# Queueing a kernel's side loads behind its weight loads, in a two-layer hybrid transformer block on one core

## The chip, the cores and the metric

The kernel runs on one NeuronCore of a Trainium2 chip. The metric is device time in microseconds (us). TensorE multiplies (PE in the profile, its weight loads PEld), VectorE (DVE), ScalarE (ACT) and GpSimd (POOL) do the elementwise work, and SyncE (SP) issues most of the transfers from HBM. Each engine executes its own queue of instructions in order. An instruction that waits holds up all that stands behind it on the same queue, and that is true of the queue in which SP issues transfers too.

## What is computed

Two layers over 512 tokens of `x` and 256 tokens of context, each 1024 wide. A layer normalises and modulates its input, projects it, feeds three branches, and merges them:

```
h = rms_norm(x, norm_w) * (1 + scale) + shift          # shift, scale, gate = silu(c) @ w_ada + b_ada
a_qkv, a_z, .., b_q, b_kv, b_z, c_qkv, c_z, merge = split(h @ w_in)
y_a = gated_head_rmsnorm(bidir_delta(...), a_z)        # branch A: gated delta rule, both directions
y_b = window_attention(...) * silu(b_z)                # branch B: attention in windows
y_c = retention_out(bidir_retention(...), c_z)         # branch C: retention, both directions
merged = sum over r of sigmoid(merge_r) * (y_r @ w_branch[r])
x = x + gate * (merged @ w_out)                        # the context likewise, in layer 0 alone
```

Branch A inverts a triangular matrix per chunk and head. After the second layer a last rms_norm gives the output.

## The kernel before

**Products.** Activations and weights are each split into a rounded part and a remainder (`hi`, `lo`), and a product is three passes on TensorE (`prod`, L261). A block of weights of 1024 x 128 is brought by `weight` (L300): SP loads it into one of two buffers `wr`, ACT rounds it into one of two `wh` (L282), POOL subtracts to get one of two `wl` in four instructions (L291). So a load of weights must wait until the block two before it has been split, and the split must wait until the product that last used its `wh` and `wl` is done. `weight` is traced with a higher priority, so that its load and split are placed well ahead of their product.

**Memory.** All other tiles are 36 slots in SBUF. `alloc` takes the slot that has been free longest, `free` gives it back. A load into a slot must wait until the last instruction that used the slot has finished. The matmul results go to eight banks in PSUM: two `px` (512 columns), one `pc` (256 columns), five general ones, `pg` (`gps`).

**Order.** The program is traced once, in the order of the code, and a planner then places each instruction on its engine's queue by priority and by the times that it reckons. On the chip that order is fixed.

**Fillers.** The projections for the gates (24 for `merge`, named `m`, and 12 named `az`, `bz`, `cz`) depend on `h` alone. `aside` (generator `self.fill`) computes them one at a time between the steps of slower chains, applies tanh (L282), and stores them to HBM as `kept`. `FILL[l]` says how many are traced in which stage: in layer 1 six beside the first inversion, 2, 4, 9 and 6 beside branch A's further stages (the 9 beside the second inversion `delta_inv`, the 6 beside the second `delta_chain`), then one in each of the eight steps of attention and one before branch C. `load` (L1243) brings a stored gate back into a slot when a branch or the merge needs it.

**The second inversion.** `delta_inv` runs 31 steps of two DVE instructions each (L288, scratch slot `ts`), then two transposes (L751, L752), sixteen DVE copies (L767) and twelve ACT copies. The ACT copies are queued behind the tanh of the filler two before (`issue_after(self.asides[-back][1])`, BACK[1] = (2, 2)). `levels` then sends bursts of small matmuls to TensorE (L795), which need all the copies.

**Branch A's end, branch B, merge.** After the second chain, `gated` (L926) brings `az`, and `branch_b` brings two tables (L1170) before its projections. The merge runs three rounds (r = 0, 1, 2 for branches A, B, C) of eight products; each is multiplied by its gate and added up. The output loop runs eight products with `w_out`, each in two halves (`out`: first half into `px`, second into `pc`), and adds the old `x` (loaded at L1381). The second halves of the last two blocks are held back until the rms of the first half has been traced.

Of the kernel before, what the change touches and what calls it, by code (L numbers as in the profile page):

```python
# [9 lines left out]
F32 = mybir.dt.float32  # L10
# [152 lines left out]
class Builder:  # L163
# [114 lines left out]
                last = i.name  # L278


    def act(self, out, in_, func, **k):
        return self.nc.scalar.activation(out, in_, func, **k)  # L282

# [10 lines left out]
    def weight(self, dram, kb=KB):  # L294
        nc = self.nc
        w = self.wr.tile([128, KB, 128], F32, name="wr")[:, 0:kb]
        hi = self.wh.tile([128, KB, 128], F32R, name="wh")[:, 0:kb]
        lo = self.wl.tile([128, KB, 128], F32R, name="wl")[:, 0:kb]
        with self.tc.high_priority(offset=WHI):
            nc.sync.dma_start(w, dram)  # L300
            self.act(hi, w, AF.Copy)
            for k in range(0, kb, 2):
                self.gtt(lo[:, k:k + 2], w[:, k:k + 2], hi[:, k:k + 2].bitcast(F32), ALU.subtract)
        return [hi[:, k] for k in range(kb)], [lo[:, k] for k in range(kb)]
# [86 lines left out]
    def ada(self, todo, ahead=1, begin=False):  # L391


        nc = self.nc

        def load(l, vec, mod, j):
            ss = [self.alloc() for _ in range(3)]
            for i in range(3):
                n = min(3, KB - 3 * i)
                nc.sync.dma_start(ss[i].f[:, 0:n * 256].rearrange("p (a b) -> p a b", a=n),  # L400
                                  self.a["wada"][l, j][:, 3 * i:3 * i + n])
            return ss

        held = deque(load(*t) for t in todo[:ahead])
        for i, (l, vec, mod, j) in enumerate(todo):
            if i + ahead < len(todo):
                held.append(load(*todo[i + ahead]))
            ss = held.popleft()
            ps = self.gps(256)
            for k in range(KB):  # L410
                g = k % 4 * 32
                nc.tensor.matmul(ps[g:g + 32], lhsT=self.csil[:, k],  # L412
                                 rhs=ss[k // 3].f[:, k % 3 * 256:k % 3 * 256 + 256],
                                 start=(k < 4), stop=(k >= 4), tile_position=(0, g))
            self.free(*ss)
            t = self.alloc()
            if begin:
                nc.vector.tensor_copy(t.f[:, 0:256], ps)
            else:
                self.act(t.f[:, 0:256], ps, AF.Copy)  # L420
            pst = self.gps(4)
            for m in range(2):
                self.mm(pst[:, m * 2:m * 2 + 2], t.f[:, m * 128:(m + 1) * 128], self.sel)
            self.free(t)
            c = slice(j, j + 9, 8) if j < 8 else slice(2 * j, 2 * j + 2)
            o, b = mod[:, c], vec[:, 8:32][:, c]
            self.tt(o, pst.rearrange("p (a b) -> p a b", b=2), b.unsqueeze(2).to_broadcast([128, 2, 2]), ALU.add)
            if j < 8:
                o = mod[:, 8 + j]
                self.stt(o, o, 1.0, vec[:, j:j + 1].to_broadcast([128, 2]), ALU.add, ALU.mult)  # L430
            else:
                nc.vector.tensor_scalar(out=o, in0=o, scalar1=0.5, scalar2=None, op0=ALU.mult)
            yield
# [732 lines left out]
    def branch_b(self, l, row, vb, last):  # L1166
        nc = self.nc
        tabs = [self.alloc(), self.alloc()]
        for i in range(2):
            nc.sync.dma_start(tabs[i].f[:, 0:512], self.a["tabs"][i])  # L1170
        cos, sin = tabs[0].f[:, 0:512], tabs[1].f[:, 0:512]
        n = SEQ if last else TOK
        kr = self.alloc()
        px, pc = self.pblk(l, "bk", True)
        self.rope(px, cos, sin, kr, 32)
        self.act(kr.f[:, SEQ:TOK], pc, AF.Copy)
        ks = []
        for g in range(2):
            kh, kl = self.alloc(True), self.alloc(True)
            src, same, other = kr.f[g * 64:g * 64 + 64], slice(g * 64, g * 64 + 64), slice(64 - g * 64, 128 - g * 64)  # L1180
            for o in (same, other):
                self.act(kh.r[o], src, AF.Copy, scale=0.125)
            for o in (same, other):
                self.stt(kl.r[o], src, 0.125, kh.f[same], ALU.mult, ALU.subtract)
            ks.append((kh, kl))
        self.free(kr)
        ns = self.st.tile([128, 8], F32, name="ns%d" % l, tag="ns")
        nc.vector.tensor_scalar(out=ns, in0=row[:, 16:24], scalar1=-1.0, scalar2=None, op0=ALU.mult)
        zs = []
        for g in range(2):  # L1190
            q = []
            for b in (2 * g, 2 * g + 1):
                px, pc = self.pblk(l, "bq%d" % b, not last)
                qr = self.alloc()
                self.rope(px, cos, sin, qr, 32)
                if not last:
                    self.act(qr.f[:, SEQ:TOK], pc, AF.Copy)
                for e in range(2):
                    t = self.alloc(True)
                    h, o = slice(e * 64, e * 64 + 64), slice(64 - e * 64, 128 - e * 64)  # L1200
                    self.act(t.r[h, 0:n], qr.f[h, 0:n], AF.Copy)
                    self.tt(t.r[o, 0:n], qr.f[h, 0:n], t.f[h, 0:n], ALU.subtract)
                    q.append(t)
                self.free(qr)
            if g:
                self.free(*tabs)
            z = [self.load("bz%d" % b, n) for b in (2 * g, 2 * g + 1)]
            for c in range(4 if last else 6):
                with self.tc.high_priority(offset=HI):
                    self.attn(c, g, q, *ks[g], vb, ns, z)  # L1210
                for _ in seq(take(self.mods, 1), take(self.fill, FILL[l][5])):
                    pass
            self.free(*q, *ks[g])
            zs.extend(z)
        return zs
# [23 lines left out]
    def load(self, nm, n):  # L1239
        while nm not in self.kept:  # L1240
            next(self.fill)
        s = self.alloc()
        self.nc.sync.dma_start(s.f[:, 0:n], self.kept[nm])  # L1243
        return s


    def layer(self, l, xs, rs, mod, vec, row, ada):
        nc = self.nc
        last = l == self.depth - 1
        n = SEQ if last else TOK  # L1250
# [75 lines left out]
        rc = self.ret_consts(l, row)  # L1326
        tabs = [self.alloc(), self.alloc()]
        for i in range(2):
            nc.sync.dma_start(tabs[i].f[:, 0:512], self.a["tabs"][2 + i])
        oc = [self.ret_head(l, h, rc, tabs, vt, last) for h in range(4)]  # L1330
        for h in range(4):
            self.tap("oc%d_%d" % (l, h), oc[h].f[:, 0:n])
# [2 lines left out]
        yc = [self.gated(l, oc[h], "cz%d" % h, nw[:, h:h + 1], not last) for h in range(4)]  # L1335
# [1 line left out]
            pass  # L1337
        m = []
        for r, y in enumerate((ya, yb, yc)):
            if r == 2:  # L1340
                y = [self.ysplit(t, n) for t in y]
            for h in range(4):
                self.tap("y%d_%d_%d" % (l, r, h), y[h][0].f[:, 0:n])
            for d in range(8):
                th = self.load("m%d_%d" % (r, d), n)
                px, pc = self.proj(self.a["wbr"][l, d, r], y, not last)
                self.stt(th.f[:, 0:SEQ], th.f[:, 0:SEQ], 1.0, px, ALU.add, ALU.mult)
                if not last:
                    self.stt(th.f[:, SEQ:TOK], th.f[:, SEQ:TOK], 1.0, pc, ALU.add, ALU.mult)
                if r:  # L1350
                    self.tt(m[d].f[:, 0:n], m[d].f[:, 0:n], th.f[:, 0:n], ALU.add)
                    self.free(th)
                else:
                    m.append(th)
            for t in y:
                self.free(*t)
# [11 lines left out]
        def out(d, w, i):  # L1368
            sl = parts[i]
            if i == 0:  # L1370
                ps = self.px.tile([128, 512], F32, name="px")[:, 0:sl.stop]
            else:
                ps = self.pc.tile([128, 512], F32, name="pc")[:, 0:256]
            self.prod(ps, w, self.hs, sl)
            x = new[d].f[:, sl]
            j = int(sl.start >= SEQ)
            self.stt(x, ps, mod[:, 16 + d, j:j + 1], x, ALU.mult, ALU.add)

        for d in range(KB):
            w = self.weight(self.a["wout"][l, d])  # L1380
            nc.sync.dma_start(new[d].f[:, 0:n], self.xd[d] if l else self.a["xT"][d][:, 0:n])  # L1381
            out(d, w, 0)
            if d < KB - 2:
                out(d, w, 1)
            else:
                held.append((d, w))
# [118 lines left out]
```

## Time and profile before

| | |
|---|---|
| median of 3 runs | 1809.99 us (1809.49 to 1810.56) |
| the profiled execution: its time | 1805.86 us |
| the profiled execution: its span, first to last instruction | 1803.7 us |
| mean granted TensorE clock | 0.984 of full speed |
| TensorE busy | 1704.5 us, 95% of the span |
| DVE, ACT, POOL busy | 1060.1, 844.6, 595.5 us |

A row of the timeline reads: start in us, length in us, engine and line, operation, output<-input, shapes, how many were merged (x), and in brackets the time that the engine sat idle before, with what ended the wait. A `q` behind an engine's name is its queue (SPq). Successive matmuls overlap, so that the last one of a row ends after the next has begun.

### The profile page before, as it was taken

Reading aid. Unit: us, or ns where it says so; the run is one execution under the profiler, and the core shown is the slowest. Engines: PE = TensorE matmul, PEld = TensorE weight load, DVE = VectorE, ACT = ScalarE, POOL = GpSimd, SP = SyncE. Lnnn points to the kernel's source line nnn. Section 1 sums busy time; section 2 is a strip of 40 time slices with the busy share of each in tenths; the row PEclk is TensorE's granted clock in tenths of the full one; section 3 lists DMA queues with packets and bytes.
Section 4 is the critical chain, followed back from the end, with each engine's and each line's share of the span. In section 5 each row is a group of like instructions: output and inputs, shape, how many; then the busy total and the mean of one; then the engine's idle time right before and its main releaser. Section 6 shows DMA issues by size and latency. Waiting matters only on the chain. (4 is left out here: it accounts for less than half of the span.)

```text
span 1803.7 us, 30670 instructions
## 1 busy us (share of the span) xinstructions
PE 1704.5 (95%) x11574; PEld 1449.5 (80%) x11574; DVE 1060.1 (59%) x2531; ACT 844.6 (47%) x2018; POOL 595.5 (33%) x739
## 2 busy tenths in 40 slices
PE   7999989999999999999999899979989999999997
PEld 3788879889877778988888697858778777888786
DVE  4668758633565464346563647966934767445653
ACT  6565545253554455222233556455354655433244
POOL 2422422312321213121453623433433422322563
PEclk9999999999999999999999999989999999999999
DMA  8211202313235234014453112201333432212552
GB/s 310 84 33 68 85 34 69 122 60 107 102 123 163 97 112 138 33 48 152 134 174 116 59 36 77 88 31 65 120 110 111 132 114 71 88 53 78 164 167 78
DMA packets 73748, 180.67 MB, mean 100 GB/s; under 512 B 8832, under 2 KB 16384, under 8 KB 73600
## 3 DMA queue, kind: packets, MB, share of 16 engines
q1 hardware_dynamic: 62144, 154.07, 26.5%
q10 hardware_dynamic: 11456, 24.65, 3.6%
q8 instruction: 91, 1.49, 0.4%
q14 instruction: 57, 0.47, 0.1%
HBM read 150.89 MB, written 27.79 MB: 99 GB/s over the span
## 5 line engine op out<-in xcount | busy, mean ns | idle before, releaser
L291 POOL TENSOR_TENSOR wl<-wr,wh 128x256 fp32r<-128x256 f32 x640 | 508.3, 825 | 1021.4 <-ACT wh L282 770.5
L261 PE MATMUL px<-hh,wh 128*128 128x512 f32 (+1 forms) x1000 | 393.0, 397 | 19.4 <-ACT wh L282 10.4
L261 PE MATMUL px<-hl,wh 128*128 128x512 f32 (+1 forms) x1000 | 393.4, 396 | 4.4 <-DVE hl L285 3.0
L282 ACT ACTIVATE wh<-wr 128x1024 fp32r<-128x1024 f32 (+1 forms) x184 | 174.3, 947 | 246.0 <-PE pc L261 101.5
L288 DVE TENSOR_TENSOR t<-t,t 128x512 f32<-128x512 f32 (+21 forms) x411 | 258.6, 630 | 41.0 <-ACT t L282 27.7
L261 PE MATMUL px<-hh,wl 128*128 128x512 f32 (+1 forms) x1000 | 263.2, 393 | 0.0
L282 ACT ACTIVATE t<-t 32x192 f32<-32x192 f32 (+10 forms) x314 | 167.4, 547 | 179.0 <-DVE t L285 127.4
L261 PE MATMUL pg<-t,t 128*128 128x128 f32 (+2 forms) x1616 | 230.3, 285 | 11.6 <-DVE t L288 11.3
L261 PEld LDWEIGHTS px<-hh,wh 128*128 128x128 f32 x1000 | 190.4, 191 | 58.4 <-ACT wh L282 11.0
L261 PEld LDWEIGHTS pg<-t,t 128*128 128x128 f32 x1616 | 205.5, 191 | 33.7 <-issue 11.4
L261 PEld LDWEIGHTS px<-hl,wh 128*128 128x128 f32 x1000 | 191.4, 191 | 41.9 <-DVE hl L285 7.5
L261 PEld LDWEIGHTS px<-hh,wl 128*128 128x128 f32 x1000 | 181.4, 190 | 33.2 <-issue 1.2
L261 PE MATMUL pc<-hh,wh 128*128 128x256 f32 x656 | 165.6, 287 | 3.7 <-DVE t L285 3.7
L261 PE MATMUL pc<-hl,wh 128*128 128x256 f32 x656 | 166.7, 289 | 2.0 <-DVE hl L285 2.0
L261 PEld LDWEIGHTS pc<-hh,wh 128*128 128x128 f32 x656 | 125.9, 192 | 8.4 <-DVE t L285 4.1
L261 PEld LDWEIGHTS pc<-hl,wh 128*128 128x128 f32 x656 | 126.2, 192 | 6.7 <-DVE hl L285 3.2
L282 ACT ACTIVATE t<-pg 128x128 f32<-128x128 f32 (+4 forms) x216 | 77.8, 384 | 110.5 <-PE pg L412 39.7
L261 PE MATMUL px<-t,wh 128*128 128x512 f32 x384 | 101.1, 401 | 4.5 <-DVE t L285 4.2
L282 ACT ACTIVATE t<-px 128x128 f32<-128x128 f32 (+2 forms) x120 | 54.7, 466 | 91.9 <-PE px L261 85.8
L261 PE MATMUL pc<-hh,wl 128*128 128x256 f32 x656 | 96.5, 287 | 0.0
L261 PEld LDWEIGHTS pc<-hh,wl 128*128 128x128 f32 x656 | 86.6, 194 | 0.9 <-issue 0.8
L261 PE MATMUL px<-t,hh 128*128 128x272 f32 (+1 forms) x384 | 86.5, 313 | 0.3 <-DVE t L285 0.3
(192 smaller groups left out, 2511.3 us busy)
## 6 DMA issues: line engine op xcount, KB each, us to landing
wr<-wblk SPq DMA_DIRECT2D x120, 512.0 KB, 3.3
t<-wada SPq DMA_DIRECT2D x48, 384.0 KB, 4.7
wr<-wbr SPq DMA_DIRECT2D x48, 256.0 KB, 2.7
m<-kept ACTq DMA_DIRECT2D x24, 384.0 KB, 2.3
t<-m SPq DMA_DIRECT2D x24, 384.0 KB, 3.4
wr<-wout SPq DMA_DIRECT2D x16, 512.0 KB, 3.3
t<-wada SPq DMA_DIRECT2D x24, 256.0 KB, 5.3
m<-kept ACTq DMA_DIRECT2D x24, 256.0 KB, 2.0
```

The lines of the kernel that those rows point to most:

```text
L261: return self.nc.tensor.matmul(out, lhsT=lhsT, rhs=rhs, start=start, stop=stop)
L282: return self.nc.scalar.activation(out, in_, func, **k)
L288: self.nc.vector.tensor_tensor(out=out, in0=in0, in1=in1, op=op)
L291: self.nc.gpsimd.tensor_tensor(out=out, in0=in0, in1=in1, op=op)
```

## The change

Four edits. `weight` keeps the instruction of its load as `self.fetch`. A new helper `bring` starts a load on SP, queued behind the load of whichever weights were traced last; it is used for stored gates (`load`), for modulation weights (`ada`, outside the start of the program), for the tables of branches B and C, and for the old `x` in the output loop. It sets an order of issue on SP's queue and waits for nothing else. The second output halves take a general bank (`gps`) in place of `pc`. Branch C's `ysplit` is traced at the start of round r = 1 in place of r = 2.

```
+    def bring(self, out, in_):
+        with self.tc.issue_after(self.fetch):
+            self.nc.sync.dma_start(out, in_)
...
         with self.tc.high_priority(offset=WHI):
-            nc.sync.dma_start(w, dram)
+            self.fetch = nc.sync.dma_start(w, dram).ins
...
-                nc.sync.dma_start(ss[i].f[:, 0:n * 256].rearrange("p (a b) -> p a b", a=n),
-                                  self.a["wada"][l, j][:, 3 * i:3 * i + n])
+                put = nc.sync.dma_start if begin else self.bring
+                put(ss[i].f[:, 0:n * 256].rearrange("p (a b) -> p a b", a=n),
+                    self.a["wada"][l, j][:, 3 * i:3 * i + n])
...
-            nc.sync.dma_start(tabs[i].f[:, 0:512], self.a["tabs"][i])
+            self.bring(tabs[i].f[:, 0:512], self.a["tabs"][i])
...
-        self.nc.sync.dma_start(s.f[:, 0:n], self.kept[nm])
+        self.bring(s.f[:, 0:n], self.kept[nm])
...
-            nc.sync.dma_start(tabs[i].f[:, 0:512], self.a["tabs"][2 + i])
+            self.bring(tabs[i].f[:, 0:512], self.a["tabs"][2 + i])
...
         for r, y in enumerate((ya, yb, yc)):
-            if r == 2:
-                y = [self.ysplit(t, n) for t in y]
+            if r == 1:
+                yc[:] = [self.ysplit(t, n) for t in yc]
...
             else:
-                ps = self.pc.tile([128, 512], F32, name="pc")[:, 0:256]
+                ps = self.gps(256)
...
-            nc.sync.dma_start(new[d].f[:, 0:n], self.xd[d] if l else self.a["xT"][d][:, 0:n])
+            self.bring(new[d].f[:, 0:n], self.xd[d] if l else self.a["xT"][d][:, 0:n])
```

## Rows read from the trace of the kernel before

**Rows 1.** Page, part 1: busy time, share of span, instructions.
```profile
PE 1704.5 (95%) x11574; PEld 1449.5 (80%) x11574; DVE 1060.1 (59%) x2531; ACT 844.6 (47%) x2018; POOL 595.5 (33%) x739
```

**Rows 2.** Waits of TensorE, whole span: total us, times, longest.
```profile
PE px L261 <- ACT wh L282: 10.7, 2, 10.4
...
PE px L261 <- ACT kept L282: 6.3, 1, 6.3
```

**Rows 3.** Chain that ended last, 1283 to 1315 us: start, us, what.
```profile
1289.60 0.86 DVE t L288
...
1297.94 0.40 DVE t L288
...
1304.71 0.33 SPq L1243
...
1310.73 8.50 PE px L261 x24
```

**Rows 4.** Waits of SP's queue, 1286 to 1311 us.
```profile
SPq L1243 <- DVE t L288: 18.2, 1, 18.2
```

**Rows 5.** Windows: length, busy PE, PEld, DVE, ACT, POOL; granted clock; DMA share; GB/s.
```profile
1293.42:1298.86 5.44, 5.44 (x26) 4.50 (x24) 5.13 (x10) 0.60 (x1) 3.50 (x4) 1.00 0.13 48
1304.46:1310.73 6.27, 0.00 (x0) 0.00 (x0) 6.16 (x14) 1.54 (x2) 0.46 (x1) 0.92 0.62 210
1310.73:1319.06 8.33, 8.33 (x25) 6.59 (x25) 4.45 (x6) 2.60 (x3) 5.78 (x8) 0.65 0.50 186
1368.00:1396.30 28.30, 28.28 (x126) 23.09 (x126) 9.91 (x29) 13.21 (x30) 14.15 (x20) 1.00 0.43 152
```

**Rows 6.** Timeline of ACT, DVE, POOL and PE, second inversion's end.
```profile
1288.28 3.65 POOL L291 TENSOR_TENSOR wl<-wr,wh 128x256 fp32r<-128x256 f32 x4 [2.13 <-PE px L261]
1307.62 7.59 DVE L767 COPY t<-t 32x192 f32<-32x192 f32 x16
1319.75 3.84 ACT L282 ACTIVATE t<-t 32x192 f32<-32x192 f32 x7
1326.03 1.02 PE L795 MATMUL pg<-t,t 32*32 32x32 f32 x96 [1.37 <-ACT t L282]
```

**Rows 7.** Timeline of SP's queue.
```profile
337.93 0.33 SPq L1243 DMA_DIRECT2D t<-az  x1
...
1377.40 0.33 SPq L300 DMA_DIRECT2D wr<-wblk  x1
...
1726.01 4.82 SPq L300 DMA_DIRECT2D wr<-wbr  x2
1732.51 35.98 SPq L300 DMA_DIRECT2D wr<-wout  x8
```

**Rows 8.** Windows around the stored gates' loads in layer 0.
```profile
325.00:365.00 40.00, 40.00 (x234) 35.52 (x233) 20.57 (x47) 13.64 (x23) 13.34 (x19) 1.00 0.34 116
```

**Rows 9.** Timeline of DVE: uses of the moved loads.
```profile
1396.99 0.75 DVE L285 SCALAR_TENSOR_TENSOR t<-pg,nw,t 128x512 f32<-128x512 f32 x1 [4.57 <-PE pg L926]
1739.29 0.67 DVE L285 SCALAR_TENSOR_TENSOR t<-t,px 128x512 f32<-128x512 f32 x1
1745.26 0.48 DVE L285 SCALAR_TENSOR_TENSOR t<-px,mod,t 128x256 f32<-128x256 f32 x1 [2.24 <-PE px L261]
```

**Rows 10.** One line's instructions: landing of L1243, then of L1381.
```profile
DMA to landing us min/median/max: 2.5/3.3/5.9
...
DMA to landing us min/median/max: 3.0/5.2/6.4
```

**Rows 11.** Timeline of ACT in the merge: the last of branch C's four splits.
```profile
1700.58 0.64 ACT L282 ACTIVATE t<-t 128x512 fp32r<-128x512 f32 x1 [1.40 <-DVE t L288]
```

**Rows 12.** Timeline of PE and DVE at the program's end.
```profile
1789.36 0.39 PE L261 MATMUL pc<-hh,wh 128*128 128x256 f32 x1 [3.10 <-DVE t L285]
1790.79 0.67 PE L261 MATMUL pg<-t,c 128*128 128x256 f32 x2
1793.05 0.48 DVE L285 SCALAR_TENSOR_TENSOR t<-pc,mod,t 128x256 f32<-128x256 f32 x1 [2.40 <-PE pc L261]
```

## The prediction

> **What bounds the kernel now.** The page's busy times come first: TensorE is busy for 1704.5 us, 95% of the span, and the next engine for 59% [rows 1]. So the time can fall only where TensorE stands idle or is clocked down, and the view to read next is the waits of TensorE. Two waits stand out there for their single longest piece: one of 10.4 us for ACT's rounding of a weight (`wh`), one of 6.3 us for ACT's tanh of a filler (`kept`) [rows 2]. The question is which of them a transfer on SP's queue causes.
>
> The 6.3 us lie at 1304.46, in layer 1's second inversion. The chain of waits tells their cause: up to 1304.7 DVE works off the steps of the inversion, then SP issues a load at L1243, then weights land, ACT rounds them, and TensorE starts at 1310.73 [rows 3]. The waits of SP's queue say what SP did meanwhile: the load at L1243, an `az` for branch A's end, waited 18.2 us for DVE's last step, because its slot is the scratch tile of the inversion [rows 4]. The next weights stood behind it on the queue, though their buffer had come free: POOL's split of the block in front ended at 1291.93 [rows 6]. ACT's rounding stood at the head of ACT's queue waiting for those weights, and the tanh that frees TensorE's bank stood behind the rounding. One early load thus stopped four engines in turn.
>
> The idle time is not all. The windows show the filler product that follows: 8.33 us at a granted clock of 0.65, against 5.44 us for the same product two places before at a clock of 1.00 [rows 5]. TensorE had been idle for 6.27 us; then it ran partly at the lower level, 1.2 GHz, before it was back at 2.4.
>
> The 10.4 us wait has no transfer in it. It lies in layer 1's first inversion, where no side load is queued; the rounding that TensorE waits for stands behind other work on ACT. The change does not touch it.
>
> **The change part by part.** *Stored gates.* `gated` is traced after the six fillers beside the second chain, so with `bring` the `az` loads stand behind the last of those fillers' weights. Layer 1 loads 2 + 4 + 6 projections and 6 + 2 + 4 + 9 + 6 fillers up to there, so that it is the 39th of its `wblk` loads; counted on SP's queue it is the one at 1377.40 [rows 7]. That is far behind 1304.7, so nothing keeps the weights waiting any more, and this is where the gain comes from.
>
> First term, TensorE: 6.27 us of idle time and 8.33 - 5.44 = 2.89 us of slow clock go [rows 5], together 9.16 us.
>
> Second term, what is late next. The small matmuls of `levels` wait for twelve ACT copies and sixteen DVE copies. The ACT copies ran from 1319.75 to 1326.03 [rows 6], behind the tanh of the delayed filler. With that product at 1304.46 to 1309.90, they come 9.36 us sooner and end at 1316.7. The DVE copies ended at 1307.62 + 7.59 = 1315.21 [rows 6], and they do not come sooner; they come later. A block of weights that arrives in time is also split in time, by POOL, in the middle of the inversion's last steps, which ran with POOL idle. Beside POOL's split of 3.65 us at 1288.28 [rows 6] a DVE step takes 0.86 us, without it 0.40 us at nearly the same size [rows 3]. One more split at half pace costs DVE 3.65 / 2 = 1.8 us, and the DVE copies end at 1317.0. The later of the two decides: the bursts start at 1317.0 in place of 1326.03, a gain of 9.0 us. (The second filler ends at about 1315.5, so TensorE waits 1.5 us there, 1.4 before.)
>
> The Trainium skill speaks of this in "GPSIMD Engine Reference", section "8. Key points": GpSimd shares its SBUF interfaces with VectorE, and they contend when the DVE instruction has two SBUF inputs. The inversion's steps have two, and the trace agrees (0.86 against 0.40 us). Without the rule the bursts would start at 1316.7 and the gain would be 9.3 us; if two splits fell into the stretch, DVE's copies would end 1.8 us later again and the gain would be 7.2.
>
> Does it last? From 1368.0 to 1396.3 TensorE is busy for 28.28 of 28.30 us [rows 5], with fillers that were left over while branch A's end goes on. Having 9 us less of them to do there, it still has 19 us of cover for that end. So the 9.0 us stay.
>
> *The same loads elsewhere.* In layer 0 an `az` stands ahead of weights too, at 337.93 [rows 7], but TensorE was busy for all 40 us around it [rows 8], since a layer 0 filler has 768 columns and lasts longer. I take no gain there. Are the moved loads late? The `az` queued at 1377.40 are used at 1396.99 [rows 9], 19.6 us later, and four land within 4 x 5.9 us even one after the other at the longest landing [rows 10]; the median is 3.3. A merge gate now stands behind the weights of the product before: for the last one 1726.01, used at 1739.29 [rows 7, 9], 13.3 us. An old `x` stands behind its own `w_out`: the first at 1732.51, used at 1745.26 [rows 7, 9], 12.8 us, against 6.4 at most to land [rows 10]. The tables are queued where branch B's first weights are, and the modulation weights of a step of attention behind the weights of the filler before. All this is hidden by products that are already split; if the cover went, one late load would cost its landing, 3 to 6 us [rows 10]. I take 0.
>
> *Output halves in general banks.* At the program's end the last second half waits 3.10 us for `pc`, until DVE has read the half before [rows 12]. In another bank it starts at 1786.26. But the rms matmul at 1790.79 stands in the middle of that product on TensorE's queue, and it waits for DVE's sum over the half before, which does not come sooner. What stood behind it, up to DVE's read at 1793.05, takes 2.26 us [rows 12]. If the planner leaves the rms matmul where it is, the gain is 0; if it moves it behind the product, up to 2.2 us. The planner reckons the product to start sooner, by the length of one DVE read, so a few matmuls more will stand ahead of it: I take 0.3, near the low end. At the layer boundary the same pattern holds; I take 0.
>
> *Branch C's split sooner.* The last of the four ACT roundings already ran at 1700.58 [rows 11]. With products of about 2.9 us the third round's eight begin near 1739 - 8 x 2.9 = 1716, so the splits were done 15 us before they were needed. No gain. If all four jumped ahead of DVE's reads, at about 0.7 us each, that would be 2.8 us in a stage where DVE has room; I take 0, with 2.8 as the worst.
>
> Sum: 9.0 + 0.3 = 9.3 us. The profiled execution took 1805.86 us with a span of 1803.7, so it would become 1796.6 with a span of 1794.4. The median of the runs stands 4.1 us above it; I carry the difference over: 1809.99 - 9.3 = **1800.7 us**, 0.5% less. (0.2%, or 3.6 us, is about what a measurement of this kernel can tell from no change.)
>
> **The rivals.** *The gain is not kept, or the block returns.* Fillers are a fixed supply; had TensorE nothing left over later, being ahead would only turn into waiting. The 28.28 us of [rows 5] speak against it. Or another moved load, waiting for its own slot, stops the weights in its new place; for that speaks that slots are given out in a fixed rotation, against it that the products there are 19 us ahead. Time: 1810.0. Chance 14%.
>
> *Slower: a rounding queued behind ACT's copies.* The planner places anew all that follows from other issue times. In the first inversion of layer 1 the rounding of a filler's weights stood behind a chain's work on ACT, and TensorE idled for 10.4 us [rows 2]. If the second inversion's next rounding is put behind the twelve ACT copies, the same price falls due there, 10.4 + 2.9 of slow clock = 13.3 us: 1800.7 + 13.3 = 1814.0. It decides as soon as the rounding for the product that runs beside `levels` comes after the copies. Against it: TensorE waits only 1.37 us at 1326.03 now [rows 6], with the same code in the same order. Chance 12%.
>
> *More than forecast.* The planner's new order happens to free the first inversion of its 10.4 us: 1800.7 - 13.3 = 1787.4; or part of it. Nothing in the change aims there. Chance 11%.
>
> **How the numbers follow.** The forecast case has 63%, its own range being 1798 (2.2 us at the end and 0.3 without POOL's cost) to 1803.5 (branch C's splits in the way). With the rivals: faster by over 0.2% 63 + 11 = 74%, within 0.2% 14%, slower 12%. The range runs from 1792 to 1811: it takes in the likeliest case and the case of no gain, and leaves out the far parts of the two others, some 18%.
>
> **What would show it.** Right: no `az` on SP's queue between 1200 and 1360; weights spaced by about 5.4 us to the inversion's end; no wait of TensorE over 2 us at the second inversion and a clock of 1.00; DVE's last steps beside POOL at 0.6 to 0.8 us; the bursts of `levels` 9 us sooner against the start of the inversion; and the stretch from those bursts to the program's end unchanged in length but for 0.3 us. Wrong: a wait of TensorE for `wh` in that place, side loads on SP that wait 5 us or more with weights behind them, DVE waiting for a gate's landing in the merge, or a stretch after `levels` that has grown by what the inversion saved.

## The result, and the profile after

| | before | after |
|---|---|---|
| median, series shown with the result | 1809.74 us (4 runs) | 1798.38 us (4 runs) |
| ratio | | 0.9934, 95% interval 0.9919 to 0.9950 |
| median, second series (`e8_all_four` below) | 1811.32 us (29 runs) | 1799.74 us (6 runs) |
| ratio | | 0.9939, interval 0.9925 to 0.9954 |
| the profiled execution: its time, its span | 1805.86, 1803.7 us | 1798.01, 1796.2 us |

The change saves 11 us, 0.6 to 0.7%. 1800.7 us had been forecast, 9.3 us less than before. The two profiled executions lie 7.5 us apart in span, less than the medians, since the one of before lies below every other run of its kernel. In the new listing, line numbers have moved: ACT's helper is L287, DVE's are L290 and L293, POOL's split is L296, the weights' load L305, the bursts of `levels` L801. All loads that go through `bring` stand at L284. The kernels of the experiments have yet other numbers, some lines off.

Where the time was won is read at the same places as before. First the page's busy times of the kernel after: TensorE has the same work [rows 1] in a shorter span.

```profile
PE 1703.9 (95%) x11574; PEld 1449.5 (81%) x11574; DVE 1062.3 (59%) x2531; ACT 844.8 (47%) x2018; POOL 593.4 (33%) x739
```

The waits of TensorE after, over the whole span. The wait for `kept` of 6.3 us [rows 2] is gone; the one of 10.3 us for `wh` is still there; the one before the second inversion's bursts of `levels`, 1.37 us before [rows 6], is now 2.5 us.

```profile
PE px L261 <- ACT wh L287: 10.6, 2, 10.3
...
PE pg L801 <- ACT t L287: 5.3, 6, 2.5
```

The timeline of SP's queue after, 1300 to 1395 us. No `az` is queued before 1369.28; seven weights run through where the blocked load stood [rows 4, 7].

```profile
1301.00 68.15 SPq L305 DMA_DIRECT2D wr<-wblk  x7
1369.28 1.55 SPq L284 DMA_DIRECT2D t<-az  x3
...
1378.06 0.32 SPq L284 DMA_DIRECT2D t<-az  x1
```

In their new place one of them waits too, as the waits of SP's queue after say: 6.7 us, for the gate's own way to DRAM, with weights behind it. The kernel before had a wait like it there, 6.5 us. TensorE goes on with fillers meanwhile, to 1388 (third of the windows below).

```profile
SPq L284 <- DMA az<-kept: 6.7, 1, 6.7
```

Then the timeline of DVE, POOL, ACT and PE at the end of the second inversion, which answers to [rows 6].

```profile
1269.54 37.35 DVE L293 TENSOR_TENSOR t<-t,t 128x31 f32<-128x31 f32 x62
...
1310.07 5.93 DVE L773 COPY t<-t 32x192 f32<-32x192 f32 x16
...
1297.79 3.19 POOL L296 TENSOR_TENSOR wl<-wr,wh 128x256 fp32r<-128x256 f32 x4 [1.94 <-ACT wh L287]
1303.23 2.87 POOL L296 TENSOR_TENSOR wl<-wr,wh 128x256 fp32r<-128x256 f32 x4 [2.25 <-ACT wh L287]
...
1308.57 0.60 ACT L287 ACTIVATE kept<-px 128x512 f32<-128x512 f32 x1 [0.70 <-PE px L261]
1310.20 3.87 ACT L287 ACTIVATE t<-t 32x192 f32<-32x192 f32 x7 [1.03 <-DVE t L758]
...
1313.97 2.40 ACT L287 ACTIVATE t<-t 32x192 f32<-32x192 f32 x5
...
1316.42 1.27 PE L801 MATMUL pg<-t,t 32*32 32x32 f32 x96 [2.45 <-ACT t L287]
```

DVE's 62 steps start at 1269.54 here and started at 1270.93 before (the row of before is below, with `e12_no_split`). The bursts start at 1316.42 here, at 1326.03 before [rows 6]. From the start of these steps to the bursts it is 46.9 us, and it was 55.1: 8.2 us less. TensorE works for 34 us without a gap, at full clock, as the windows of the kernel after show in their first line (columns as in [rows 5]); the second line is the 10 us behind the first burst, the third the fillers beside branch A's end.

```profile
1279.86:1313.97 34.11, 34.11 (x151) 27.93 (x149) 32.47 (x58) 13.41 (x19) 20.30 (x25) 1.00 0.42 141
1316.42:1326.42 10.00, 9.80 (x319) 8.25 (x319) 1.66 (x3) 4.19 (x10) 2.78 (x4) 0.66 0.24 84
1359.90:1388.00 28.10, 28.08 (x125) 22.86 (x125) 9.45 (x27) 12.67 (x28) 14.12 (x20) 1.00 0.53 185
```

That is one place. The boundary between the layers is another, and the sum had 0 there; the experiments come to it.

### The profile page after: what moved, and what is told of

Read it like the earlier page. It is cut to its first block, busy times and chain, and to the rows that moved or that the text cites. A ratio compares the mean times of both kernels' runs of the same rounds, so it can differ in the third digit from the quotient of the medians.

```text
span 1796.2 us, 30682 instructions
## 1 busy us (share of the span) xinstructions
PE 1703.9 (95%) x11574; PEld 1449.5 (81%) x11574; DVE 1062.3 (59%) x2531; ACT 844.8 (47%) x2018; POOL 593.4 (33%) x739
## 5 line engine op out<-in xcount | busy, mean ns | idle before, releaser
L296 POOL TENSOR_TENSOR wl<-wr,wh 128x256 fp32r<-128x256 f32 x640 | 506.6, 821 | 1016.6 <-ACT wh L287 773.6
L261 PE MATMUL px<-hh,wh 128*128 128x512 f32 (+1 forms) x1000 | 392.9, 397 | 13.2 <-ACT wh L287 10.3
L293 DVE TENSOR_TENSOR t<-t,t 128x512 f32<-128x512 f32 (+21 forms) x411 | 264.3, 644 | 41.0 <-ACT t L287 28.5
L287 ACT ACTIVATE wh<-wr 128x1024 fp32r<-128x1024 f32 (+1 forms) x184 | 174.3, 947 | 220.9 <-PE pc L261 83.1
L287 ACT ACTIVATE t<-t 32x192 f32<-32x192 f32 (+10 forms) x314 | 167.4, 546 | 186.7 <-DVE t L290 144.9
L261 PEld LDWEIGHTS pg<-t,t 128*128 128x128 f32 x1616 | 205.8, 191 | 33.4 <-issue 11.2
L261 PEld LDWEIGHTS px<-hh,wh 128*128 128x128 f32 x1000 | 190.8, 191 | 52.0 <-ACT wh L287 11.2
L261 PE MATMUL pc<-hl,wh 128*128 128x256 f32 x528 | 133.7, 288 | 0.9 <-DVE hl L290 0.8
L261 PE MATMUL pc<-hh,wh 128*128 128x256 f32 x528 | 133.4, 287 | 0.2 <-ACT hh L287 0.2
L287 ACT ACTIVATE t<-pg 128x128 f32<-128x128 f32 (+4 forms) x216 | 77.8, 384 | 108.9 <-PE pg L418 39.7
L261 PEld LDWEIGHTS pc<-hl,wh 128*128 128x128 f32 x528 | 101.2, 192 | 4.7 <-DVE hl L290 1.5
L261 PEld LDWEIGHTS pc<-hh,wh 128*128 128x128 f32 x528 | 101.1, 192 | 4.2 <-issue 1.2
L287 ACT ACTIVATE t<-px 128x128 f32<-128x128 f32 (+2 forms) x120 | 54.6, 465 | 91.2 <-PE px L261 85.3
L261 PEld LDWEIGHTS px<-t,wh 128*128 128x128 f32 x384 | 71.2, 191 | 19.1 <-DVE t L290 3.1
L261 PE MATMUL pg<-hh,wh 128*128 128x256 f32 (+1 forms) x264 | 79.7, 326 | 3.0 <-DVE t L290 2.9
```

What stands on the lines that cost most here:

```text
L261: return self.nc.tensor.matmul(out, lhsT=lhsT, rhs=rhs, start=start, stop=stop)
L293: self.nc.vector.tensor_tensor(out=out, in0=in0, in1=in1, op=op)
L296: self.nc.gpsimd.tensor_tensor(out=out, in0=in0, in1=in1, op=op)
```

## The experiments

All ratios are to the kernel before, run in the same series.

**The gates alone, and the gates put back.** Two runs look at the first edit from both sides. `e1_gates_only` is the kernel before with `bring` in `load` and nowhere else:

```
-        self.nc.sync.dma_start(s.f[:, 0:n], self.kept[nm])
+        self.bring(s.f[:, 0:n], self.kept[nm])
```

> The kernel before, with only the loads of the stored gates (az and the gates of the merge) queued behind the last traced weights. Theory (one az load at the head of SP's queue, waiting for the inversion's scratch slot, stops the weights and with them ACT and TensorE): nearly all of the gain comes with this part alone. The bursts of levels start 8 to 9.6 us sooner after the second inversion's start, TensorE has no wait over 3 us there, and the ratio to the kernel before is 0.994 to 0.996 (7 to 11 us less). Rival (the gain is the sum of many small moves of the planner, or comes from the other loads, the banks or the split): a third of the gain or less, ratio 0.998 to 1.000.

Measured: 0.9956 (0.9944 to 0.9968), 8.0 us, interval 5.8 to 10.1. From the start of DVE's steps at 1273.29 to the bursts at 1320.17 it is 46.9 us, as in the kernel after.

`e2_gates_back` is the kernel after with that line alone as it was before.

> The kernel after, with only the stored gates' loads issued directly again; other loads, banks and split stay changed. Theory (blocked az): the wait of SP's queue for DVE's last inversion step comes back with some 18 us, TensorE's idle time of some 6 us in the second inversion with it, and the time goes back to that of before but for what the end of the program gives: ratio 0.999 to 1.000. Rival (other parts carry the gain): ratio 0.994 to 0.996 stays.

Measured: 0.9963 (0.9950 to 0.9976). The stall is back, as its waits of SP and then its timeline of PE show:

```profile
SPq L1249 <- DVE t L293: 18.1, 1, 18.1
```

```profile
1312.15 0.79 PE L261 MATMUL px<-hh,wh 128*128 128x512 f32 x1 [5.88 <-ACT kept L287]
```

But the time did not go back to that of before: 6.7 us of gain were left (4.4 to 9.1). So the theory holds for its place and not for the total. Something else in the change was worth more than the 0.3 us of the sum.

**The wait, not the place.** `e3_own_scratch` moves no load. The inversion's scratch gets a tile of its own, and the slot that it used to take is still taken out of the rotation, unused.

```
-        ts = self.alloc()
+        hole = self.alloc()
+        ts = self.st.tile([128, 256], F32, name="ts")
...
-        self.free(ts)
+        self.free(hole)
```

> The kernel before, no load moved; the inversion's scratch lies in a tile of its own, and the slot that it took from the rotation is still taken and given back, but nothing writes or reads it. So the az load is still early, but the slot that it takes has no late reader. Theory (it is the wait of the az load for that slot, not its early place on the queue, that costs the time): the 18.2 us wait of SP goes, TensorE's 6.27 us go, and the ratio is 0.994 to 0.996. Rival (the place of the az transfer itself costs, by the bytes that go ahead of the weights, or the gain is a matter of new order): the az loads stay ahead of the weights, and the ratio is 0.998 to 1.000.

Measured: 0.9952 (0.9940 to 0.9964), 8.7 us. Its timeline of SP's queue has the `az` ahead of the twelve weights, not blocked; the kernel before has it between them [rows 3, 4].

```profile
1243.67 0.33 SPq L300 DMA_DIRECT2D wr<-wblk  x1
1246.72 0.33 SPq L1244 DMA_DIRECT2D t<-az  x1
1261.64 63.73 SPq L300 DMA_DIRECT2D wr<-wblk  x12
```

An early `az` does no harm here. One that waits for a slot at the head of the queue does, and it makes no difference which of the two is mended.

**The banks.** `e4_banks_only` has only the second output halves in general banks:

```
-                ps = self.pc.tile([128, 512], F32, name="pc")[:, 0:256]
+                ps = self.gps(256)
```

> The kernel before, with only the second output halves in general banks. Theory (the rms matmul stands in the middle of the last product, so that the free bank gives only the matmuls ahead of it): 0.3 to 0.8 us, ratio 0.9995 to 1.000, with the wait of 3.10 us at the end replaced by one of some 2.4 us further on. Rival (the bank wait was all cost): 2 to 3 us, ratio 0.9985.

Measured: 0.9967 (0.9954 to 0.9980), 6 us, twenty times the term of the sum. Both expected sizes were missed, though the wait at the end moved as expected. Two more runs split the edit by layer. The line below is that of `e9_banks_l0`, where layer 0 alone gets general banks; `e10_banks_l1` has them in the last layer alone.

```
-                ps = self.pc.tile([128, 512], F32, name="pc")[:, 0:256]
+                ps = self.pc.tile([128, 512], F32, name="pc")[:, 0:256] if last else self.gps(256)
```

> The kernel before, with the second output halves in general banks in layer 0 alone. Theory (formed on the trace of the kernel with the banks alone): at the boundary between the layers VectorE sets the pace for some 24 us; with the bank free its splits of h are done 0.9 us sooner, and TensorE has no slow stretch behind them, so that the first small matmuls of layer 1 come 2 to 3 us sooner. Ratio 0.998 to 0.999. Rival (the boundary gives nothing, as predicted; the whole gain is at the program's end): 0.9995 to 1.0005.

> The kernel before, with the second output halves in general banks in layer 1 alone. Theory: the program's end becomes 1 to 2.5 us shorter, ratio 0.9985 to 0.9995; with layer 0's part it adds up to what the banks gave alone (0.9967). Rival (the end gives all of the 0.9967): 0.9965 to 0.9975. Rival as predicted: 0.3 us, ratio 0.9998.

Measured: layer 0 alone 0.9976 (0.9966 to 0.9985), 4.3 us (2.7 to 6.2), a little more than its theory had; layer 1 alone 1.0000 (0.9990 to 1.0011), nothing, where 1 to 2.5 us had been expected. The two add to less than the 6 us of both layers (3.6 to 8.3), within the intervals. At the program's end the trace of `e10_banks_l1` has the wait of 3.10 us for `pc` [rows 12] replaced by one for the rms matmul, with seven matmuls behind it:

```profile
1797.61 1.22 PE L261 MATMUL pg<-t,c 128*128 128x256 f32 x2 [2.41 <-DVE t L288]
1798.27 2.06 PE L261 MATMUL pg<-hh,wl 128*128 128x256 f32 x7
```

The gain is at the boundary. Below are its windows, first of the kernel before, then of the one after. They run from the second half's rms matmul (TensorE's start behind its wait, 1011.25 and 1011.95), over 14 us, to the end of the second projection of layer 1, and to its first small matmuls (L606, now L612).

```profile
1011.25:1025.25 14.00, 11.13 (x41) 7.42 (x41) 14.00 (x12) 10.50 (x19) 13.98 (x12) 0.88 0.29 93
1025.25:1038.88 13.63, 11.42 (x48) 9.03 (x49) 13.12 (x18) 7.40 (x14) 11.69 (x14) 0.87 0.09 24
1038.88:1084.55 45.67, 44.61 (x299) 40.59 (x299) 22.00 (x48) 26.81 (x87) 8.66 (x14) 1.00 0.14 45
```

```profile
1011.95:1025.95 14.00, 11.55 (x37) 7.47 (x37) 14.00 (x12) 9.78 (x17) 14.00 (x12) 0.76 0.29 92
1025.95:1037.10 11.15, 9.95 (x47) 7.18 (x46) 10.69 (x16) 8.19 (x16) 10.15 (x13) 1.00 0.11 29
1037.10:1083.29 46.19, 44.89 (x300) 40.91 (x300) 23.19 (x52) 27.04 (x87) 9.79 (x15) 1.00 0.13 44
```

What the reader is to see: in the first 14 us DVE is busy for all of them, in both kernels, and POOL with it. This is a stage where DVE and POOL set the pace, while they prepare layer 1's `h`. The second stretch shrinks from 13.63 to 11.15 us; the third is 0.5 us longer. The steps of `h` stand in another order on ACT, DVE and POOL, and with them the products on TensorE. The timeline of DVE, of before and then of after, has an example: the read of the second half, and with it all that needs the sum, starts 6.0 us behind the start of the rms matmul before and 4.9 after, with three steps to `hl` just ahead of it in place of one to `hl` and one other.

```profile
1012.71 4.63 DVE L285 SCALAR_TENSOR_TENSOR hl<-t,mod,hh 128x512 fp32r<-128x512 f32 x3
1017.25 0.47 DVE L285 SCALAR_TENSOR_TENSOR t<-pc,mod,t 128x256 f32<-128x256 f32 x1
```

```profile
1013.51 1.75 DVE L290 SCALAR_TENSOR_TENSOR hl<-t,mod,hh 128x512 fp32r<-128x512 f32 x1
1015.19 1.76 DVE L290 SCALAR_TENSOR_TENSOR t<-t,mod,t 128x512 f32<-128x512 f32 x1
1016.88 0.47 DVE L290 SCALAR_TENSOR_TENSOR t<-pg,mod,t 128x256 f32<-128x256 f32 x1
```

The waits of TensorE over both stretches, of before and then of after, give the idle part of it: those for `hl` fall from 5.0 to 3.2 us.

```profile
PE px L261 <- DVE hl L285: 3.0, 4, 1.0
PE pc L261 <- DVE hl L285: 2.0, 5, 0.4
```

```profile
PE px L261 <- DVE hl L290: 2.4, 4, 1.2
...
PE pc L261 <- DVE hl L290: 0.8, 2, 0.5
```

From the rms matmul to the small matmuls it is 73.3 us before and 71.3 after. In the eight traces with general banks in layer 0 it is 71.3 us in each, in the four without (before, `e1_gates_only`, `e3_own_scratch`, `e10_banks_l1`) 73.3 to 74.4. So 2.0 to 3.1 of the 4.3 us are placed. Two things change there together, the order of the steps and TensorE's clock. In the 13 us that begin 14 us behind the rms matmul the granted clock is 1.00 in all eight traces with general banks, 0.87 in three of those without, and 0.77 in the fourth, `e1_gates_only`, which has the 74.4 us. How much the new order saves by itself and how much by the clock no run here separates. What is left of the 4.3 us is not placed: the 95 to 99 us behind the small matmuls, up to the 10.3 us wait, overlap between the two groups.

**Two parts for four.** `e11_two_parts` is the kernel before with the gates' loads behind the weights and general banks in layer 0, without the other loads, the split and layer 1's banks.

> The kernel before with two of the edits alone: the stored gates' loads queued behind the weights, and the second output halves in general banks in layer 0 only. If these two carry the whole change, the ratio is 0.9956 x 0.9976 = 0.993, as with all four edits (0.9939 and 0.9934). Rival (the other loads, the split or layer 1's banks carry something that no run alone showed): 0.9945 or above.

Measured: 0.9937 (0.9923 to 0.9951). `e8_all_four` is the kernel after once more, in a second series:

> The kernel after, all four edits, in one series with the next three. If the gates' part (0.9956 measured alone) and the banks' part (0.9967 alone) stand in different places, they add: 0.9956 x 0.9967 = 0.9923, some 14 us. If one hides part of the other, the ratio stays at 0.9934 or above, 12 us or less.

Measured: 0.9939 (0.9925 to 0.9954), so that the parts do not add to 14 us. The two parts carry the change; the others are worth nothing that these intervals, 5 us wide, can tell, and the sum had them at 0 and 0.3. Alone the two parts give 8.0 and 4.3 us; the two together give 11.4, all four edits 11.0 and 11.9 in the two series.

**What POOL's splits cost.** In `e12_no_split` the fillers beside layer 1's second inversion have no low part split on POOL; TensorE's third pass reads the rounded weights again. (`bare` is true beside that inversion alone.)

```
...
-        lo = self.wl.tile([128, KB, 128], F32R, name="wl")[:, 0:kb]
+        lo = hi if self.bare else self.wl.tile([128, KB, 128], F32R, name="wl")[:, 0:kb]
...
-            for k in range(0, kb, 2):
+            for k in range(0, 0 if self.bare else kb, 2):
```

> The kernel after, but the fillers beside layer 1's second inversion don't get their low parts split on GpSimd: their third pass reads the rounded weights again, so these gates are computed wrongly while TensorE's work is the same. Theory (GpSimd's splits slow VectorE's steps, and two of them in the last steps held the bursts of levels back): VectorE's steps beside the fillers take 0.4 us in place of 0.8 us at 128x112, its transposes come at least 3.2 us sooner against the fillers, TensorE's wait of 2.4 us before the bursts goes, and with it the slow clock in the bursts: 2.5 to 4 us less than the kernel after, ratio to the kernel before 0.9915 to 0.9925. Rival (the bursts wait for ScalarE's copies behind the rounding and the tanh, whatever VectorE does): the wait stays, ratio 0.9934 to 0.994.

Measured: 0.9920 (0.9902 to 0.9939); beside the kernel after the intervals overlap, so that a gain over it is not shown. The size fits the theory, the trace does not. Here are DVE's 62 steps of the kernel before and of this one, then this one's copies on DVE and ACT and its bursts.

```profile
1270.93 33.71 DVE L288 TENSOR_TENSOR t<-t,t 128x31 f32<-128x31 f32 x62
```

```profile
1268.90 23.38 DVE L293 TENSOR_TENSOR t<-t,t 128x31 f32<-128x31 f32 x62
...
1295.45 5.01 DVE L775 COPY t<-t 32x192 f32<-32x192 f32 x16
...
1308.88 0.58 ACT L287 ACTIVATE kept<-px 128x512 f32<-128x512 f32 x1
1309.36 3.83 ACT L287 ACTIVATE t<-t 32x192 f32<-32x192 f32 x7
...
1315.55 1.02 PE L803 MATMUL pg<-t,t 32*32 32x32 f32 x96 [2.23 <-ACT t L287]
```

The steps take 23.38 us with no split beside them, 33.71 with six (before) and 37.35 with eight (after). DVE is through at 1300.46, and yet the bursts start at 1315.55 and TensorE's wait of 2.2 us is still there. The ACT copies are queued behind the tanh of a filler, at 1308.88, and follow TensorE's fillers, not DVE. From that tanh to the bursts it is 6.7 us, and 7.9 in the kernel after (1308.57 to 1316.42), where the copies also waited 1.03 us for DVE's transposes. So 14 us on DVE were worth 1.2 us from tanh to bursts. From the inversion's start to the bursts it is 46.65 us, 0.2 less than in the kernel after. Behind the bursts, too, this kernel has a shorter stretch (next section).

**The wait that is left.** `e7_back1` goes for the 10.3 us wait in layer 1's first inversion: the twelve copies there are queued behind the last filler in place of the one before the last.

```
-BACK = ((2, 3), (2, 2))
+BACK = ((2, 3), (1, 2))
```

> The kernel after, with the twelve copies of layer 1's first inversion queued behind the last filler beside it in place of the one before the last, so that the rounding of the weights that TensorE waits 10.3 us for stands ahead of the copies on ScalarE. Theory (the wait comes from that order alone): the 10.3 us go and with them a stretch of slow clock, and what is lost is the later start of levels, up to one filler: 4 to 10 us less than the kernel after, ratio to the kernel before 0.988 to 0.991. Rival (the inversion's end is what counts there, the idle time is only its shadow): no gain or a loss, ratio 0.9934 to 0.998.

Measured: 1.0004 (0.9993 to 1.0015): all of the change's gain is lost, more than either side had expected. The wait itself fell to 3.7 us. The waits of TensorE from 1178 to 1320 us, and then the timeline with the first bursts of both inversions, say what came for it; the line below them is the first inversion's in the kernel after.

```profile
PE pg L612 <- DVE t L290: 5.2, 2, 4.1
PE px L261 <- ACT wh L287: 3.7, 1, 3.7
```

```profile
1209.96 1.02 PE L801 MATMUL pg<-t,t 32*32 32x32 f32 x96 [2.47 <-ACT t L287]
...
1327.66 1.50 PE L801 MATMUL pg<-t,t 32*32 32x32 f32 x96 [9.50 <-ACT t L287]
```

```profile
1198.80 1.02 PE L801 MATMUL pg<-t,t 32*32 32x32 f32 x96 [0.16 <-DVE t L773]
```

The first bursts start 11.2 us later than in the kernel after, the second 11.2 us later too (1316.42), with 117.6 to 117.7 us between them in both kernels. In the other four traces that have no blocked load and have their splits it is 117.0 to 117.4 us. The chain from the first inversion to the second has its own length, and whatever delays its head moves its end. TensorE does its fillers sooner against the chain; at the second inversion it is through with those that stand ahead of the bursts, and waits 9.5 us there. The edit took 6.6 us off the wait by moving the copies back, and the copies are the head of that chain; it does not tell what the wait would be worth to an edit that leaves them where they are.

## Why the prediction came out as it did

*The blocked load: right in place, in mechanism and nearly in size.* The gates' part had been reckoned at 9.0 us. It measured 8.0 alone (5.8 to 10.1), and 8.7 with the other cure. Most signs came: no `az` between 1200 and 1369, weights every 5.1 to 5.8 us, the fillers without a gap at full clock. Two did not come as named. TensorE waits over 2 us at the second inversion, 2.45, before the bursts; and a side load waits over 5 us with weights behind it, the `az` at 1378, as one did before. Neither took the gain back.

*What is late next: the price was right, one count was wrong, and so was the engine that ends last.* One more split of POOL had been put into DVE's last steps, for 1.8 us. There were two, at 1297.79 and 1303.23, and the steps took 37.35 - 33.71 = 3.6 us longer, exactly twice as much; the case of two splits had been named, at 7.2 us. It came out at 8.2. DVE's copies ran in 5.93 us in place of 7.59 [rows 6], since less of POOL's work fell beside them, and would have allowed 8.6; ACT's copies end last, at 1316.37 against 1316.00. That ACT's copies read DVE's transposes and so wait for them, 1.03 us, had not been seen. `e12_no_split` shows that DVE's pace matters for the bursts by little more than that, 1.2 us. Two smaller steps of the working do not hold, and nothing hangs on them: ACT's copies were to come 9.36 us sooner where the sum beside it gives 9.16, and four `az` loads one after the other at 5.9 us would take 23.6 us, more than the 19.6 us that they were given (at the median of 3.3 us it is 13.2). In the kernel after DVE never waits for one of them.

*Behind the bursts 1.0 us is given back.* "So the 9.0 us stay" was a little too good. From the first burst to the end of the 1.74 us wait of attention it is 93.9 us before (1326.03 to 1419.94) and 94.9 after (1316.42 to 1411.35). The same length is 94.7 to 95.2 in the six traces without the block that have their splits, and 93.6 to 94.2 in the other four with the block; in `e12_no_split` it is 93.5. After, the first 10 us of it run at a clock of 0.66 (second of the windows above), TensorE having waited 2.45 us; but `e1_gates_only` had the same wait and, as its window shows, a clock of 1.00, and lost nearly as much; `e11_two_parts` likewise, with 2.44 us, 1.00 and 95.0.

```profile
1320.17:1330.17 10.00, 7.85 (x319) 6.29 (x319) 1.66 (x3) 4.37 (x10) 2.79 (x4) 1.00 0.26 84
```

Nor is it the wait alone: `e12_no_split` waits 2.23 us and has 93.5. So the clock is not the cause, or not alone; it stays open. To the program's end the whole stretch had been forecast unchanged but for 0.3 us; it is 477.7 us before and 479.8 after. But `e8_all_four`, the same kernel, has 482.5, so that two traces alone do not give this difference.

*The output halves: the place that was priced gave nothing, the one that was waved through gave 4.3 us.* The program's end had been reckoned at 0.3 us and gave 0.0 (interval -2.0 to +1.8): the rms matmul stands in the middle of the product, as was argued. "At the layer boundary the same pattern holds; I take 0" is the step that failed. The bank wait there is 0.6 us, in the timeline of TensorE of the kernel before:

```profile
1007.70 0.39 PE L261 MATMUL pc<-hh,wh 128*128 128x256 f32 x1 [0.58 <-DVE t L285]
```

With the same edit DVE's, POOL's and ACT's steps for layer 1's `h` come in another order, in a stage where DVE is busy for 14.00 of 14.00 us, and TensorE's clock behind it is 1.00 in place of 0.87. That the gain is the edit's and lies in layer 0 is shown by `e9_banks_l0` and `e10_banks_l1`; that the order is its cause is argued from the traces. At the program's end no product waits behind.

*The other loads, and branch C's split:* reckoned at 0, and `e11_two_parts` measures the kernel without them as fast as with them, within its interval.

*The total.* 9.0 + 0.3 + 0 had been summed to 9.3; alone the parts measured 8.0 + 0 + 4.3, and together 11.0 to 11.9. The forecast's 1800.7 is 2.3 us from the median. That it is so near is in part luck: a term that came out 1 us too large stands against one of 4.3 us that was taken as 0.

*The rivals.* The block did not return. The rounding was not put behind the copies in the second inversion (it ran at 1306.80, ahead of them, and the wait there is 2.45 us, not 10.4). The first inversion kept its 10.3 us. Its price of 13.3 us, which stood in two of the rivals, had been taken from TensorE's lost time alone; `e7_back1` took 6.6 us of that wait away and gained nothing by it, so that no run bears the price out.

## What to carry to other kernels

A load that waits for a slot at the head of a shared queue blocks everything behind it, so ask of each early load who reads its slot last; to free the slot does as well as to move the load. Price an edit in every place where it acts, and look there for the engine that is busy all the time: at a boundary where DVE was full, an edit that also changed the order of its steps was worth 4.3 us, seven times the wait that could be read off. And an idle engine is only worth filling if the chain beside it does not get longer by it: take the length from one fixed step of the chain to the next (here 117.6 us, whether TensorE had idled 10.3 us ahead of it or 3.7) before setting a price on the idle.

## What the hardware showed that was not expected

DVE's steps beside POOL: 23.38 us for 62 steps with no split beside them, 33.71 with six, 37.35 with eight. That is 1.72 and 1.75 us more for each split, which itself takes 2.83 to 3.65 us. The prediction had the rate right from two rows, but not that six splits already cost the kernel before 10 us of DVE's time in this inversion. "GPSIMD Engine Reference", section "8. Key points", of the Trainium skill says that the two engines contend when DVE reads two operands from SBUF; these runs agree, and the 1.7 us for each split are its size here. DVE's sixteen copies of the same inversion, which read one operand, slow down too: 5.01 us with POOL idle, 5.93 with one split beside their start, 7.59 with POOL busy for their last 4.9 us.

The clock behind a short wait: with TensorE idle for 2.43 to 2.45 us before the bursts the next 10 us had a granted clock of 0.66 in three traces (after, `e3_own_scratch`, `e8_all_four`), and with 2.44 and 2.47 us 1.00 in two (`e11_two_parts`, `e1_gates_only`). TensorE had been busy without a gap, at a clock of 1.00, for 17.5 us ahead of the wait in all five. The length of the wait alone does not tell which of the two comes.
